# Bidirectional gated DeltaNet scan on one core: the second direction's operands moved to the other half of the partitions, its products queued in turn with the first's, and the state scaling on GpSimd

## The chip, the cores and the metric

The kernel runs on one core of one Trainium2 chip. The metric is device time in microseconds of one launch; the time before the change is the median of three runs.

## The reference

One layer of a hybrid model: 512 latent tokens and 256 context tokens of width 1024 go through a modulated RMS norm and one wide input projection, then through two mixers side by side (windowed attention, and a bidirectional gated delta rule), a gated merge, an output projection and a squared-ReLU MLP. All is fp32. The change is in the delta rule, cut to what matters:

```python
def gated_delta_chunked(q, k, v, g_log, beta, s0):
    # chunks of 64 tokens, 8 heads of 64; per chunk: G = cumsum(g), T = I + b * decay * k k^T
    ...
    def step(S, xs):
        w_c, uv_c, qd_c, intra_c, kt_c, gl_c = xs
        u = uv_c - jnp.einsum('bhck,bhkv->bhcv', w_c, S)
        o = jnp.einsum('bhck,bhkv->bhcv', qd_c, S) + jnp.einsum('bhij,bhjv->bhiv', intra_c, u)
        S = jnp.exp(gl_c)[..., None, None] * S + jnp.einsum('bhck,bhcv->bhkv', kt_c, u)
        return S, o
```

It runs forward and, on flipped inputs, backward; first over the 4 context chunks from a zero state, then over the 8 latent chunks from the states reached. The outputs of the two directions are added. So there are 12 steps, each of them one after the other, with two directions that do not depend on each other.

## The kernel before

Weights come from memory in 512 KB tiles, are split into a high and a low part (line 259 on ScalarE, line 266 on VectorE), and each large product is done as three matmuls. Between these large products the kernel runs the smaller ones of attention and of the delta rule.

A latent tile of state, values or products holds 128 partitions by 256 columns: the 8 heads are four columns of blocks (q = 0 to 3) by two halves of the partitions (64 each). A small product takes its two operands from one half of the partitions and writes to one half of a PSUM bank.

`chain_step(d, step)` is one step of one direction d, a generator with three phases:

- phase 0: the state products z = k S and, in latent steps, q S (line 1152), then R = z * eG - v / 2 on VectorE (lines 1156, 1157);
- phase 1: u = (inverse) R (line 1164), then uk = u * tb on VectorE (line 1170) and, in latent steps, a copy `us` (line 1174) and the scaled readout `zq` of q S (line 1176, one per head column) on ScalarE;
- phase 2: the new state's products (line 1185) and the inner outputs (line 1189), the old state scaled by its decay on ScalarE (line 1199, one per head column), the new state on VectorE (line 1201), and the output sums (lines 1208 to 1215).

`steps` runs the two directions phase by phase: all of direction 0's phase, then all of direction 1's. Between phases the caller puts other matmuls, the fill: `filler()` makes the attention branch's products (line 1073) and 14 gate tiles of 24 matmuls (line 1028), 432 matmuls in all. In the context scan, `weave` mixes the steps with the inverse of the latent chunks' matrices (`invert`, lines 856 and 857 on VectorE), 144 fill matmuls, and `rest` (normalising the queries, turning values and keys token-major). Then four transposes (`back`, line 867) and two `combine`s (lines 877 and 887, results copied at 896 to 899, zeros by GpSimd at 900 and 901) finish the latent inverses XA, and the query products (line 777) with VectorE, ScalarE and GpSimd (lines 1278 to 1289) make the masks IA; 144 fill matmuls stand between. The latent scan follows with `FILL[3]` = 8, 7 and 3 fill matmuls after the phases 0, 1 and 2.

`late_mod` makes 32 rows of the second modulation (line 1094, one VectorE product over a 512 KB tile each); `run_late` calls it in many places, in the latent scan once per step. `tok_major` (line 915) writes the token-major values VTM and keys KTM.

The order on each engine is fixed when the program is built: by program order, except that an instruction whose inputs are not ready by the builder's own estimate of the times is passed by later ones that are. Every engine then runs its queue in order. `add_manual_dep` adds an order to that without a wait.

## Time and profile before

| | us |
|---|---|
| median of 3 runs (911.4 to 913.39) | 912.83 |
| profiled execution | 911.22 |
| its span | 909.5 |
| TensorE matmul busy | 879.4 (97%) |
| VectorE busy | 585.4 (64%) |
| ScalarE busy | 454.9 (50%) |
| GpSimd busy | 25.2 (3%) |

The two scans, with what lies between them, take the stretch from 294 to 467 us of the span. In rows of the profile, "L1164" is line 1164 of the kernel, `x32` is a count of instructions, the first number of a row in order of time is its start in the span, the second its length, and `[0.74 <-DVE m L1157]` says that the engine stood idle for 0.74 us until that instruction released it. Each small fp32 product of 64x64x64 leaves two matmul records, so the 16 products of line 1164 in one step (8 per direction) are 32 records, and the 32 of line 1152 in a latent step are 64. In a table of stretches each row gives start:end, length, and the busy time of each engine with the number of instructions.

### The profile page before, as it was taken

Reading aid. Unit: us, or ns where it says so; the run is one execution under the profiler, and the core shown is the slowest. Engines: PE = TensorE matmul, PEld = TensorE weight load, DVE = VectorE, ACT = ScalarE, POOL = GpSimd, SP = SyncE. Lnnn points to the kernel's source line nnn. Section 1 sums busy time; section 2 is a strip of 40 time slices with the busy share of each in tenths; the row PEclk is TensorE's granted clock in tenths of the full one; section 3 lists DMA queues with packets and bytes.
Section 4 is the critical chain, followed back from the end, with each engine's and each line's share of the span. In section 5 each row is a group of like instructions: output and inputs, shape, how many; then the busy total and the mean of one; then the engine's idle time right before and its main releaser. Section 6 shows DMA issues by size and latency. Waiting matters only on the chain.

```text
span 909.5 us, 16844 instructions
## 1 busy us (share of the span) xinstructions
PE 879.4 (97%) x7082; PEld 704.7 (77%) x7082; DVE 585.4 (64%) x999; ACT 454.9 (50%) x819; POOL 25.2 (3%) x40
## 2 busy tenths in 40 slices
PE   8999999999899999999999999999999999999998
PEld 5668777867677787777678789888888888888886
DVE  3578799887778997677867988941654335324511
ACT  6588755476568786465663445630452134113400
POOL 0010001010000002010000000000000000000000
PEclk9999999999999999999999999999999999999999
DMA  8671455533001133633316773640553224322111
GB/s 355 262 230 21 92 117 120 112 71 58 13 13 35 56 110 94 207 98 95 117 37 219 245 245 135 227 144 1 188 157 95 70 73 150 103 69 79 38 47 46
DMA packets 30460, 105.59 MB, mean 116 GB/s; under 512 B 3760, under 2 KB 4400, under 8 KB 29360
## 3 DMA queue, kind: packets, MB, share of 16 engines
q1 hardware_dynamic: 28368, 97.18, 33.1%
q0 software_dynamic: 2016, 7.34, 5.0%
q8 instruction: 55, 0.90, 0.4%
q14 instruction: 21, 0.17, 0.1%
HBM read 102.41 MB, written 2.10 MB: 115 GB/s over the span
## 4 chain that ended last, share of the span: by engine, by line
PE 80%; DVE 10%; ACT 5%; issue 2%; DMA 1%; SPq 0%; DVEq 0%; ACTq 0%
PE banks L319 16%; PE banks L317 16%; PE banks L318 16%; PE banks L1028 9%; PE banks L424 5%; PE banks L1073 2%; PE banks L429 2%; PE banks L586 2%; PE banks L596 1%; PE banks L1164 1%; ACT m L148 1%; PE banks L662 1%; PE banks L1185 1%; PE banks L1152 1%; PE banks L210 1%
## 5 line engine op out<-in xcount | busy, mean ns | idle before, releaser
L317 PE MATMUL banks<-m,m 128*128 128x512 f32 (+1 forms) x600 | 223.6, 377 | 2.6 <-DVE m L643 1.6
L318 PE MATMUL banks<-m,m 128*128 128x512 f32 (+1 forms) x600 | 224.5, 376 | 0.1
L319 PE MATMUL banks<-m,m 128*128 128x512 f32 (+1 forms) x600 | 224.2, 376 | 0.0
L259 ACT ACTIVATE m<-wr 128x1024 fp32r<-128x1024 f32 x68 | 71.8, 1059 | 155.1 <-PE banks L318 74.0
L317 PEld LDWEIGHTS banks<-m,m 128*128 128x128 f32 x600 | 111.8, 188 | 26.0 <-ACT m L323 2.8
L318 PEld LDWEIGHTS banks<-m,m 128*128 128x128 f32 x600 | 112.5, 188 | 21.9 <-DVE m L324 1.5
L319 PEld LDWEIGHTS banks<-m,m 128*128 128x128 f32 x600 | 112.4, 188 | 21.3 <-issue 1.2
L266 DVE TENSOR_TENSOR m<-wr,m 128x1024 fp32r<-128x1024 f32 x68 | 82.8, 1224 | 62.8 <-ACT m L259 31.2
L1028 PE MATMUL banks<-m,wh 128*128 128x512 f32 x320 | 104.5, 405 | 1.5 <-issue 0.8
L1471 DVE SCALAR_TENSOR_TENSOR m<-banks,modT,m 128x512 f32<-128x512 f32 x32 | 24.0, 750 | 105.3 <-PE banks L319 105.3
L259 ACT ACTIVATE wh<-wr 128x1024 fp32r<-128x1024 f32 (+1 forms) x58 | 54.6, 941 | 50.6 <-issue 11.4
L424 PE MATMUL banks<-m,wh 128*128 128x512 f32 (+1 forms) x320 | 75.9, 374 | 1.2 <-DVE m L823 1.2
L1028 PEld LDWEIGHTS banks<-m,wh 128*128 128x128 f32 x320 | 58.0, 188 | 14.2 <-issue 1.0
L1028 PE MATMUL banks<-m,wl 128*128 128x512 f32 x160 | 64.7, 405 | 0.0
L424 PEld LDWEIGHTS banks<-m,wh 128*128 128x128 f32 x320 | 53.0, 189 | 11.5 <-issue 1.9
L266 DVE TENSOR_TENSOR wl<-wr,wh 128x1024 fp32r<-128x1024 f32 (+1 forms) x44 | 45.2, 1028 | 16.6 <-ACT wh L259 16.5
L184 ACT ACTIVATE m<-m 128x512 fp32r<-128x512 f32 (+1 forms) x56 | 34.8, 629 | 38.1 <-DVE m L1454 21.5
L185 DVE TENSOR_TENSOR m<-m,m 128x512 fp32r<-128x512 f32 (+1 forms) x56 | 38.3, 689 | 21.6 <-ACT m L184 21.3
L1094 DVE SCALAR_TENSOR_TENSOR m<-wa,m 128x1024 f32<-128x1024 f32 x32 | 39.0, 1223 | 12.6 <-DMA wa<-in_wada 7.4
L317 PE MATMUL banks<-m,wh 128*128 128x512 f32 (+1 forms) x120 | 42.0, 352 | 0.0
L319 PE MATMUL banks<-m,wl 128*128 128x512 f32 (+1 forms) x120 | 42.0, 351 | 0.0
L318 PE MATMUL banks<-m,wh 128*128 128x512 f32 (+1 forms) x120 | 41.8, 349 | 0.0
(241 smaller groups left out, 1371.8 us busy)
## 6 DMA issues: line engine op xcount, KB each, us to landing
wr<-in_wm SPq DMA_DIRECT2D x64, 512.0 KB, 3.7
wr<-in_win SPq DMA_DIRECT2D x38, 512.0 KB, 3.7
wa<-in_wada SPq DMA_DIRECT2D x32, 512.0 KB, 4.1
m<-in_wada SPq DMA_DIRECT2D x8, 1024.0 KB, 12.3
wl<-in_win POOLq DMA_DIRECT2D x14, 512.0 KB, 5.7
m<-in_xT SPq DMA_DIRECT2D x8, 512.0 KB, 5.6
wr<-in_wbr SPq DMA_DIRECT2D x16, 256.0 KB, 2.6
wr<-in_wout SPq DMA_DIRECT2D x8, 512.0 KB, 4.6
```

The costliest lines, as they stand in the source:

```text
L184: A.activation(r32(hi), src, AF.Copy)
L185: (eng or V).tensor_tensor(r32(lo), src, hi, op=ALU.subtract)
L259: h = A.activation(r32(hi), raw, AF.Copy)
L266: V.tensor_tensor(r32(lo), raw, hi, op=ALU.subtract)
L317: PE.matmul(acc, w[0][:, k, :], xhi, start=(start and i == 0), stop=False)
L318: PE.matmul(acc, w[0][:, k, :], xlo, start=False, stop=False)
L319: PE.matmul(acc, w[1][:, k, :], xhi, start=False, stop=(stop and i == n - 1))
L424: PE.matmul(a, w[0][:, k, :], x, start=(k == 0 and x is xs[k][0]), stop=False)
L429: PE.matmul(a, w[1][:, k, :], xs[k][0], start=False, stop=(k == KT - 1))
L1028: PE.matmul(acc.ap, w[x][:, k, :], hx[k][y], start=(k == p == 0), stop=(k == KT - 1 and p == 2))
L1094: V.scalar_tensor_tensor(t.ap, wa, 0.5, scr.ap, op0=ALU.mult, op1=ALU.mult, accum_out=modT[:, grp, j:j + 1])
L1471: V.scalar_tensor_tensor(xn_[ct], acc.ap, modT[:, 3, ct:ct + 1], xn_[ct], op0=ALU.mult, op1=ALU.add)
```

## The change

- Direction 1's inverses (`XAb` in `combine`) are written to the other half of the partitions; its values come from a copy `VTS` of the values with the halves exchanged (`swapped`, two DMAs on GpSimd's queue for each group of four chunks); z of k S and R lie in the other half too (`r2[i ^ x ^ d]`, `eGs` for direction 1). u, uk, the state and the outputs stay where they were.
- The products of line 1164, and in context steps those of line 1152, are yielded one head column at a time, so direction 0's and direction 1's stand in turn in the queue. In latent steps the state products stay together per direction.
- Since direction 1's q S now lies in the half where it does not belong, its readout is eight ScalarE operations of 64 partitions instead of four of 128.
- The scaling of the old state is one GpSimd product of 128x256, issued right after R, instead of four ScalarE operations in phase 2.
- In the second half of the latent steps the sum of the two directions' outputs, its squares and their sum are done after phase 1 of the next step (`add_up`). These sums and the rows of `late_mod` are ordered behind the last chain operation on VectorE (`behind`, `mark`). `late_mod` writes in place.
- `FILL[3]` becomes 7, 6, 5; the first latent phase 0 goes before the second group of query products; the latent scan makes four late rows instead of eight, two come after the gate tiles and six instead of four in the branch products; `rest` turns the values before it normalises the queries; the context scan is preceded by the exchanged copy and 12 fill matmuls. In `combine` direction 1's own columns are always copied.

```diff
-FILL = 144, 36, 36, (8, 7, 3)
+FILL = 144, 36, 36, (7, 6, 5)
...
         for a in range(2):
             lo, hi = quad(a, 0), quad(a, 1)
+            blo, bhi = quad(1 - a, 0), quad(1 - a, 1)
             A.activation(XAf[hi, :, HC:], XTf[hi], AF.Copy)
-            A.activation(XAb[hi, :, HC:], XTb[hi], AF.Copy)
+            A.activation(XAb[blo, :, :HC], XTb[lo], AF.Copy)
+            A.activation(XAb[bhi, :, HC:], XTb[hi], AF.Copy)
             A.activation(XAf[lo, :, HC:], xo[lo], AF.Copy)
-            A.activation(XAb[hi, :, :HC], xo[hi], AF.Copy)
+            A.activation(XAb[bhi, :, :HC], xo[hi], AF.Copy)
...
+    def swapped(g):
+        VTS[g] = alloc(1024, True)
+        for a in range(2):
+            G.dma_start(out=VTS[g][64 * a:64 * a + 64], in_=VTM[g][64 * (1 - a):64 * (1 - a) + 64])
...
-            t = alloc(1024)
-            V.scalar_tensor_tensor(t.ap, wa, 0.5, scr.ap, op0=ALU.mult, op1=ALU.mult, accum_out=modT[:, grp, j:j + 1])
-            t.free()
+            op = V.scalar_tensor_tensor(wa, wa, 0.5, scr.ap, op0=ALU.mult, op1=ALU.mult, accum_out=modT[:, grp, j:j + 1])
+            behind(op)
...
-        vt = VTM[c // 4][:, c % 4 * 256:(c % 4 + 1) * 256]
-        if S is not None:
-            for q in range(4):
+        vt = (VTS if d else VTM)[c // 4][:, c % 4 * 256:(c % 4 + 1) * 256]
+        for q in range(4):
+            if S is not None:
                 for x, src in enumerate((kT, qT) if lat else (kT,)):
                     for i, r in enumerate(r2):
-                        PE.matmul(z[r2[i ^ x], x * 512 + q * HD:x * 512 + (q + 1) * HD], src[q][r, col(c):col(c) + CH],
+                        PE.matmul(z[r2[i ^ x ^ d], x * 512 + q * HD:x * 512 + (q + 1) * HD], src[q][r, col(c):col(c) + CH],
                                   S[r, q * HD:(q + 1) * HD], start=True, stop=True)
+            if not lat:
+                yield
...
-            V.tensor_tensor(hv(R), hv(z[:, 0:256]), bc(eG[:, d, m4], HD), op=ALU.mult)
-            V.scalar_tensor_tensor(R, vt, -0.5, R, op0=ALU.mult, op1=ALU.add)
+            V.tensor_tensor(hv(R), hv(z[:, 0:256]), bc((eGs if d else eG)[:, d, m4], HD), op=ALU.mult)
+            mark[0] = V.scalar_tensor_tensor(R, vt, -0.5, R, op0=ALU.mult, op1=ALU.add)
+            if not last:
+                se = alloc(256)
+                G.tensor_tensor(hv(se.ap), hv(S.ap), bc(egl[:, d, m4], HD), op=ALU.mult)
...
-            for r in r2:
-                PE.matmul(u[r, q * HD:(q + 1) * HD], XA[lat][d][r, (cl * 4 + q) * CH:(cl * 4 + q + 1) * CH],
-                          R[r, q * HD:(q + 1) * HD], start=True, stop=True)
+            for i, r in enumerate(r2):
+                rr = r2[i ^ d]
+                PE.matmul(u[r, q * HD:(q + 1) * HD], XA[lat][d][rr, (cl * 4 + q) * CH:(cl * 4 + q + 1) * CH],
+                          R[rr, q * HD:(q + 1) * HD], start=True, stop=True)
+            yield
...
-                A.activation(zq[:, q * HD:(q + 1) * HD], z[:, 512 + q * HD:512 + (q + 1) * HD], AF.Copy,
-                             scale=eGs[:, d, c * 4 + q:c * 4 + q + 1])
+                for o, r in ((r2[1], r2[0]), (r2[0], r2[1])) if d else ((slice(0, P),) * 2,):
+                    A.activation(zq[o, q * HD:(q + 1) * HD], z[r, 512 + q * HD:512 + (q + 1) * HD], AF.Copy,
+                                 scale=(eG if d else eGs)[r, d, c * 4 + q:c * 4 + q + 1])
...
-                se = alloc(256)
-                for q in range(4):
-                    A.activation(se[:, q * HD:(q + 1) * HD], S[:, q * HD:(q + 1) * HD], AF.Copy,
-                                 scale=egl[:, d, c * 4 + q:c * 4 + q + 1])
...
+    def behind(op):
+        if mark[0]:
+            tc.add_manual_dep(op.ins, mark[0].ins.name, nosync, reason="behind the chain")
+
+    def add_up():
+
+        while after:
+            dst, b, cl = after.pop(0)
+            behind(V.tensor_tensor(dst, dst, b.ap, op=ALU.add))
+            A.activation(b.ap, dst, AF.Square)
+            V.tensor_reduce(oss[:, cl], hv(b.ap), axis=AX.X, op=ALU.add)
+            b.free()
...
-            for _ in range(3):
-                for g in both:
-                    next(g, None)
+            for n, parts in enumerate((1 if step >= NCC else 5, 5, 1)):
+                for _ in range(parts):
+                    for g in both:
+                        next(g, None)
+                if n == 1:
+                    add_up()
                 yield
...
+    swapped(0)
     to_tokens(KTM, kT, 0)
+    run_fill(12)
...
+        if g:
+            run_both(FPAUSE)
+            next(scan)
+        run_both(FILL[2] - (1 + g) * FPAUSE)
...
-    for n, _ in enumerate(steps(range(NCC, NC_))):
+    for n, _ in enumerate(scan, 1):
         run_fill(FILL[3][n % 3])
-        if n % 3 == 2:
+        if n % 3 == 1 and n < 3 * NCL // 2:
             run_late(1)
...
+    run_late(2)
     H.free()
...
-        run_late(ct % 2)
+        run_late(ct < 6)
```

More of the change, by code (lines that the diff above doesn't have):

```diff
@@ L917, in tok_major @@
             pt.free()
-    KTM, VTM = [None] * 3, [None] * 3
+    KTM, VTM, VTS = [None] * 3, [None] * 3, [None] * 3
     qT = []
@@ L1220, in steps @@
             both = [chain_step(d, step) for d in range(2)]
-            for _ in range(3):
-                for g in both:
-                    next(g, None)
+            for n, parts in enumerate((1 if step >= NCC else 5, 5, 1)):
[4 more added lines that the diff above has]
+                    add_up()
                 yield
+        add_up()
     def rest():
-        for q in range(4):
-            l2n(qT[q].ap, HD ** -0.5, ((0, SEQ),), epsc4)
-            yield
         for g in (1, 2):
@@ L1234, in rest @@
             t.free()
+        for q in range(4):
+            l2n(qT[q].ap, HD ** -0.5, ((0, SEQ),), epsc4)
+            yield
         for g in (1, 2):
@@ L1243, in tile_layer @@
         pass
-    for b in KTM[:1] + VTM[:1] + XA[0]:
+    for b in KTM[:1] + VTM[:1] + VTS[:1] + XA[0]:
         b.free()
@@ L1253, in tile_layer @@
         xr.append(alloc(1024))
-        back(xa[d][:, :, :HC], 1 + d, d == 1)
-        back(v3(xr[d].ap), 1 + d, d == 0)
+    xr.append(alloc(1024))
+    xr3 = [v3(b.ap) for b in xr]
+    back(xa[0][:, :, :HC], 1, False)
+    back(xr3[0], 1, True)
+    back(xr3[2], 2, True)
+    back(xr3[1], 2, False)
     X[1][0].free()
-    xr3 = [v3(b.ap) for b in xr]
     for g in range(2):
@@ L1265, in tile_layer @@
         b.free()
+    swapped(1)
+    swapped(2)
     IA = [alloc(2048, True), alloc(2048, True)]
+    scan = steps(range(NCC, NC_))
     ia = [v64(b.ap) for b in IA]
@@ L1302, in tile_layer @@
         pass
-    for b in kT + qT + KTM[1:] + VTM[1:] + XA[1] + IA + zb + Sb[0] + Sb[1]:
+    for b in kT + qT + KTM[1:] + VTM[1:] + VTS[1:] + XA[1] + IA + zb + Sb[0] + Sb[1]:
         b.free()
```

18 lines of the change are left out of this document (8 added, 10 removed).

## The prediction

> **What bounds the kernel now.** I read the page first, then the table of the stages around the two scans, then the chain of work that ended last and the order of time inside single steps. The page says who carries the span.
>
> ```profile
> span 909.5 us, 16844 instructions
> PE 879.4 (97%) x7082; PEld 704.7 (77%) x7082; DVE 585.4 (64%) x999; ACT 454.9 (50%) x819; POOL 25.2 (3%) x40
> PE 80%; DVE 10%; ACT 5%; issue 2%; DMA 1%; SPq 0%; DVEq 0%; ACTq 0%
> ...
> wl<-in_win POOLq DMA_DIRECT2D x14, 512.0 KB, 5.7
> ```
>
> TensorE carries it, so only two things count: less TensorE work, or fewer holes between its instructions. The scans lie in these stretches: context scan, combines and query products, latent scan, and what follows.
>
> ```profile
> 294.00:354.30 60.30, 59.88 (x556) 46.04 (x556) 56.53 (x106) 48.85 (x110) 2.24 (x5) 1.00 0.28 84
> 354.30:394.30 40.00, 39.33 (x893) 31.22 (x892) 22.54 (x33) 19.92 (x35) 5.49 (x10) 1.00 0.53 164
> 394.30:467.00 72.70, 67.15 (x1402) 51.78 (x1393) 53.86 (x123) 44.13 (x150) 1.48 (x2) 1.00 0.31 95
> ```
>
> Columns after the length: busy time of PE, PEld, DVE, ACT, POOL, then the granted clock (1.00 throughout). The context scan has TensorE and VectorE full at once (59.88 and 56.53 of 60.30); the latent scan has TensorE with 5.5 us of open holes, and VectorE at 74%. The chain prices the products:
>
> ```profile
> 308.91 1.08 PE banks L1152 x32
> ...
> 346.80 7.63 PE banks L1028 x32
> ...
> 360.79 4.85 PE banks L1028 x20
> ...
> 408.07 1.08 PE banks L1164 x32
> ...
> 413.41 1.09 PE banks L1152 x64
> ...
> 424.06 2.07 PE banks L1028 x8
> 426.13 1.08 PE banks L1164 x32
> 427.21 1.82 PE banks L1028 x7
> ...
> 453.21 1.08 PE banks L1164 x32
> ...
> 474.71 11.38 PE banks L1028 x49
> ```
>
> The reader should see that 64 records and 32 records cost the same. The 64 (state products of a latent step, L1152) use all four pairings of input half and output half; the 32 (L1164, and L1152 in the context steps) use only two, each half onto itself. So a pairing is a lane, and two lanes stand empty in L1164. A latent step without holes is 1.09 + 2.07 + 1.08 + 1.82 + 1.09 (new state and outputs, also 64 records) + three fill matmuls (0.78 at the rate of the seven) = 7.9 us. Measured from the L1164 at 408.07 to the one at 453.21, five steps take 45.14, or 9.03 each: 1.1 us of holes per step, some 9 us in eight steps.
>
> **The change part by part.**
>
> *Lanes, latent scan.* The second direction's inverses, values and R lie in the other half, and its L1164 products are queued one head after another with the first's: all four pairings in one stretch. 64 records' worth of lanes for 32 + 32: each step's L1164 goes from 1.08 to 1.09 / 2 = 0.54. Eight steps: **-4.3 us**. Nothing hides this; it is TensorE's own time. Bounds 0 (no overlap at all) and -4.3. I take the full value, because L1152 already shows the four-lane rate with the same sizes.
>
> *Lanes, context scan.* Four L1164 and three L1152 groups, 7 x 0.54 = 3.8 us of TensorE. But VectorE sets the end there: the inverse's two-input products (L856, L857) and four transposes lead into the first combine.
>
> ```profile
> L857 DVE TENSOR_TENSOR m<-m,m x60: 191/398/656, 138.1 to 341.4; 128x168 f32<-128x168 f32 x4, 128x30 f32<-128x30 f32 x2, 128x58 f32<-128x58 f32 x2, 128x84 f32<-128x84 f32 x2
> 351.89 2.12 DVE L867 STREAM_TRANSPOSE m<-m 128x1024 f32<-128x1024 f32 x1
> ```
>
> The last transpose ends at 354.0; the 32 fill matmuls from 346.80 end at 354.43, just when the combine's products can start. A TensorE that arrives 3.8 us earlier waits for VectorE, unless later fill is pulled ahead (it was in the latent scan: the code asks for 8, 7, 3 and single steps ran 8, 8, 2). VectorE has 3.8 us idle in this stretch (60.30 - 56.53). I take **-1.0**, nearer to the VectorE row; bounds -3.8 and, if GpSimd gets in its way (rival below), +4.2.
>
> *Holes by late modulation rows.* L1094 takes 1.22 us of VectorE in the middle of the chain:
>
> ```profile
> 441.64 1.22 DVE L1094 SCALAR_TENSOR_TENSOR m<-wa,m 128x1024 f32<-128x1024 f32 x1
> 443.12 0.74 DVE L1156 TENSOR_TENSOR m<-banks,eg 128x256 f32<-128x256 f32 x2
> 444.25 1.15 PE L1164 MATMUL banks<-m,m 64*64 64x64 f32 x32 [0.74 <-DVE m L1157]
> ...
> 461.23 1.22 DVE L1094 SCALAR_TENSOR_TENSOR m<-wa,m 128x1024 f32<-128x1024 f32 x1
> 462.37 0.42 DVE L1157 SCALAR_TENSOR_TENSOR m<-m,m 128x256 f32<-128x256 f32 x1
> 462.85 0.68 PE L1164 MATMUL banks<-m,m 64*64 64x64 f32 x16 [0.35 <-DVE m L1157]
> ```
>
> At 441.64 it stands ahead of R and TensorE sits 0.74; at 461.23 it splits R of the second direction and costs 1.22 less the 0.68 of the first direction's products. After the change four instead of eight are in the scan, each ordered behind the last chain operation, as are the output sums, which move one phase on. Behind uk they have the run of six fill matmuls plus the first half of the 64 records, some 2.2 us, before VectorE is wanted. Bounds 0 and -3.0 (four hits of about 0.75); I take **-2.0**. The four moved rows (and four more 512 KB loads later) lie beside the gate tiles' 49 matmuls and the branch products, TensorE unbroken for 11.38 us; without that cover they cost 4 x 1.22 = 4.9. The in-place product frees arena space and costs the same 1.22.
>
> *State scaling to GpSimd, output scaling doubled for one direction.*
>
> ```profile
> 412.69 2.02 ACT L1199 ACTIVATE m<-m,egl 128x64 f32<-128x64 f32 x8 [0.82 <-DVE m L1201]
> 414.62 1.71 ACT L1176 ACTIVATE m<-banks,eGs 128x64 f32<-128x64 f32 x8
> 418.65 0.79 ACT L1174 ACTIVATE m<-banks 128x256 f32<-128x256 f32 x2 [2.32 <-DVE m L1170]
> 379.47 0.73 PE L1028 MATMUL banks<-m,wh 128*128 128x512 f32 x2 [0.67 <-ACT m L148]
> 388.79 1.06 ACT L259 ACTIVATE wh<-wr 128x1024 fp32r<-128x1024 f32 x1
> 397.86 0.74 POOL L1288 MEMSET m<- 32x512 f32 x1 [10.00 <-DVE m L1285]
> ```
>
> ScalarE loses eight L1199 (2.02 us per step) and gains four L1176 (half of 1.71, 0.86). The loss frees the hole of 0.67 at 379.47, where eight L1199 from 375.8 held up the weight split and the tanh behind it: **-0.7**, bounds 0 and -2.0. The gain lies where it is wanted: twelve L1176 (2.57) and two L1174 (0.79) must end before the new state's products, 1.82 + 0.54 + 1.6 = 4.0 us after the state products. That leaves 0.6 us; a weight split (1.06) that falls in there, with its tanh (0.6), overruns by 1.0. Six tiles, some of them twice unlucky: **+2.0**, bounds 0 and 8 x 0.86 = +6.9.
>
> The GpSimd product (128x256, two inputs) has no row here. Nearest rows: 0.74 for its memset of 512 elements, 0.42 for VectorE's 128x256 product. I take 0.7. It starts when the state is there and is wanted a whole step later (7 us, two products 1.4): **0** in the latent scan as long as one product stays under 3 us; above that each microsecond costs two per step.
>
> *Ahead of the scans.* The swapped values come by DMA on POOL's queue behind sixteen evictions.
>
> ```profile
> 293.57 6.31 ACT L915 ACTIVATE m<-banks 64x256 f32<-64x256 f32 x16
> 294.10 1.04 PE L1164 MATMUL banks<-m,m 64*64 64x64 f32 x16 [0.89 <-ACT m L915]
> ...
> 299.47 0.68 PE L1164 MATMUL banks<-m,m 64*64 64x64 f32 x16
> ```
>
> The eight of the values end near 296.7; with the queue's 5.7 us (bound from above, those are 512 KB from memory; here 256 KB in two) the first L1164 starts at 301 to 303 instead of 294.1 and 299.5. Twelve more fill matmuls (2.8 us) and eight transposes of the reordered rest stand before it; behind it on POOL waits only the first state product, wanted at 318. **+0.5**, bounds 0 and +3. The four later DMAs have 30 us to land. Five more copies in the combines (0.6 each) lie under 20 fill matmuls, 4.85 us; without that cover 3.0.
>
> *Start of the latent scan.* Its first state products now go before the second half of the query products, so R no longer waits for the masks' building, but uk does.
>
> ```profile
> 395.48 1.28 DVE L1278 TENSOR_TENSOR m<-m,banks 128x512 f32<-128x512 f32 x2
> 397.39 1.83 DVE L1285 COPY m<-m 32x512 f32<-32x512 f32 x4
> 400.48 1.15 PE L1164 MATMUL banks<-m,m 64*64 64x64 f32 x32 [1.74 <-DVE m L1157]
> ```
>
> VectorE needs 1.28 + 0.68 + 1.83 = 3.8 us there; TensorE has 0.54 + 1.6 us before it wants uk, where before it had 13 fills and lost 1.74. **+0.5**, bounds -1.7 and +2.3.
>
> The sum: -4.3 - 1.0 - 2.0 - 0.7 + 2.0 + 0.5 + 0.5 = **-5.0 us**. The profiled execution took 911.22 (span 909.5), 1.6 under the median 912.83; from 911.22 the sum gives 906.2, and the same difference on the median **907.8**. About 1.8 us (0.2%) is what the runs can tell from no change.
>
> **The rivals.**
>
> *All of it stays.* The lanes give 4.3 + 3.8, pulled-ahead fill covers VectorE in the context scan, and 6 of the 9 us of holes go: -14, **899**. For it: every hole named has VectorE or ScalarE work in front of it that is moved. Against it: the filled VectorE of the first stretch, and L266, which is not ordered behind the chain and at 434.26 split R just as L1094 did.
>
> *GpSimd gets in VectorE's way (slower).* Place: the state product beside VectorE operations with two inputs from SBUF: L856/L857 in the context scan, R's second operation and L266 in the latent one. Price: if each holds VectorE for its own 0.7 us, 6 x 0.7 = 4.2 on the full VectorE ahead of the combine and 14 x 0.7 = 9.8 in the chain; with the first whole and a third of the second on the path, +7.5: **915**; all of it, 922. It decides from 0.25 us per product (5.0 / 20) on. For it: VectorE has no slack in the first stretch, and the order on TensorE is fixed ahead of time. Against it: POOL ran only memsets and DMA issues there, so the trace has no overlap to show; and in the latent scan the product would run beside the state products, when VectorE idles. The Trainium skill has the rule behind this rival: SBUF — State Buffer, "Who interferes with whom", says that a VectorE instruction with two SBUF inputs contends with a GpSimd instruction that reads SBUF and that the loser blocks for the whole instruction. No run so far shows it. The skill's GPSIMD Engine Reference, "Elementwise — side-by-side cycle accounting", gives about 2.6 cycles per element for two inputs, which is an estimate of 0.55 us plus dispatch for 256 elements; by it the full price would be 11 us, not 14.
>
> *The lanes are given back.* With the directions in turn, the first direction's uk waits for the second direction's R, so L1170 no longer overlaps the products; a step would lose on VectorE (0.42 + 0.42 after the products) what TensorE saved, and ScalarE's twelve readouts take the rest: -4.3 falls away, **912**. For it: R of both takes 1.5 us (four operations, 0.74 a pair) against 1.82 of cover, so any insertion breaks it. Against it: six fills (1.6) stand behind L1164, and uk for both (0.74, as two L1156 of that size), the second copy (half of 0.79) and some 0.3 of latency are 1.45.
>
> **How the numbers follow.** The forecast (903 to 911.0) 0.57; all of it 0.15; GpSimd 0.15; given back 0.13. Faster by over 0.2% (under 911.0): 0.57 + 0.15 = 0.72; within 0.2%: 0.13; slower: 0.15. The range 898.5 to 915.5 reaches the first rival's time and the smaller price of the second; outside lie about half of the GpSimd case and a few hundredths below. The forecast's own range is 903 to 911.
>
> **What would show it.** L1164's stretch at 0.54 us for 32 records, and L1152 likewise in the context steps (right); 1.08 in both (given back at the root). The five-step pace at about 8.3 to 8.5 us, where 7.5 would be all of it and 9 none. No L1094 between L1201 and L1157. In the first stretch, TensorE idle ahead of L877 with L867 as the releaser, 2 to 3 us. The POOL products at 0.5 to 0.9 us each; VectorE's L856/L857 grown in mean above 0.39 and 0.40 us would be contention. I am wrong if the latent scan's TensorE holes grow (waits of L1185 on ScalarE L1176 or L1174 over 3 us in sum), or if the new state waits for GpSimd.

## The result

The changed kernel is slower: 920.28 us (median of 6 runs, 919.46 to 925.19) against 912.60 us of the kernel before, timed beside it (910.39 to 914.42); ratio 1.0089 (95% interval 1.0072 to 1.0106). The forecast was 907.8, with 898.5 to 915.5 as its range. The profiled execution took 919.46 us.

The page after, with the rows that answer to those of before:

```profile
span 917.7 us, 16870 instructions
...
PE 880.7 (96%) x7082; PEld 702.6 (77%) x7082; DVE 587.3 (64%) x999; ACT 452.7 (49%) x776; POOL 42.4 (5%) x66
...
PE 74%; DVE 13%; ACT 7%; issue 3%; DMA 3%; SPq 0%; DVEq 0%; ACTq 0%
```

TensorE's busy time is 1.3 us up although its small products use two lanes more; that is the clock (below), since an execution of nearly the same kernel at full clock (e6) has 876.8. In the chain ScalarE and the DMA have each gained 2 points.

The next fence is the table of stretches after: context scan (from its first product to the first combine), combines and query products (to the last query product), latent scan (to the last inner outputs); then from the last fill matmul to the first matmul of the second norm, and from there to the last of it. Line 1157 after is line 1152 before, 1164 and 1165 are 1156 and 1157, 1176 is 1164, 1183 is 1170, 1187 is 1174, 1190 is 1176, 1199 is 1185, 1203 is 1189, 1099 is 1094, 1034 is 1028; 1168 is the new product on GpSimd.

```profile
296.49:360.98 64.49, 61.15 (x568) 45.63 (x568) 60.95 (x110) 44.55 (x88) 10.38 (x15) 1.00 0.34 99
360.98:406.00 45.02, 42.26 (x956) 32.99 (x956) 22.06 (x35) 23.80 (x43) 7.20 (x13) 0.96 0.51 160
406.00:469.70 63.70, 60.79 (x1332) 45.83 (x1320) 48.10 (x111) 42.51 (x121) 8.82 (x14) 1.00 0.25 77
488.96:558.62 69.66, 66.82 (x344) 55.78 (x343) 58.37 (x92) 27.68 (x39) 0.00 (x0) 1.00 0.81 262
558.62:569.04 10.42, 9.83 (x74) 9.34 (x75) 10.15 (x23) 5.58 (x12) 0.00 (x0) 1.00 0.26 72
```

And the same stretches of the kernel before, cut at the same events:

```profile
294.10:354.37 60.27, 59.95 (x557) 46.01 (x557) 56.50 (x106) 48.82 (x110) 2.31 (x5) 1.00 0.28 84
354.37:394.21 39.84, 39.17 (x893) 31.17 (x892) 22.47 (x33) 19.76 (x34) 5.42 (x10) 1.00 0.53 164
394.21:466.22 72.01, 66.46 (x1405) 51.21 (x1393) 53.12 (x121) 44.22 (x150) 1.48 (x2) 1.00 0.32 96
485.70:552.10 66.40, 66.38 (x347) 56.04 (x346) 55.92 (x87) 27.04 (x38) 0.00 (x0) 1.00 0.76 247
552.10:561.39 9.29, 8.95 (x69) 8.45 (x68) 9.17 (x22) 5.75 (x13) 0.00 (x0) 1.00 0.20 56
```

The latent scan is 8.3 us shorter and the two stretches ahead of it are 4.2 and 5.2 longer: 12 fill matmuls (2.8 us) and a group of state products (1.2 us) were moved into them, and the granted clock of the second is 0.96. The three together are 1.1 us longer. What is lost beyond doubt stands further down: behind the scans, where the change touches only the late rows and the placing of buffers, 66.40 us have become 69.66 and 9.29 have become 10.42. A further 2.4 us are lost ahead of the scans (first product of line 1176 at 296.49 instead of 294.10); e6 below, whose only further edit lies behind the scans, does not lose them.

One latent step after, and the start of the same product five steps later:

```profile
420.77 0.61 POOL L1168 TENSOR_TENSOR m<-m,egl 128x256 f32<-128x256 f32 x1
...
422.98 2.56 ACT L1190 ACTIVATE m<-banks,eg 64x64 f32<-64x64 f32 x8
...
424.15 0.69 PE L1176 MATMUL banks<-m,m 64*64 64x64 f32 x32
424.78 0.73 PE L1034 MATMUL banks<-m,wh 128*128 128x512 f32 x2
...
426.18 1.06 ACT L259 ACTIVATE wh<-wr 128x1024 fp32r<-128x1024 f32 x1
...
427.36 0.33 PE L1199 MATMUL banks<-m,m 64*64 64x64 f32 x4 [0.92 <-ACT wh L259]
...
466.18 0.69 PE L1176 MATMUL banks<-m,m 64*64 64x64 f32 x32
```

The 32 records of line 1176 now leave TensorE after 0.63 us (424.15 to 424.78) instead of 1.08, and five steps take 42.03 us, 8.41 each instead of 9.03. They do so in six of the eight latent steps. In the other two the products of the two directions stand apart or mostly behind one another, and take 1.22 us (two times 0.61) and 1.24:

```profile
415.79 0.68 PE L1176 MATMUL banks<-m,m 64*64 64x64 f32 x16
...
448.86 1.31 PE L1176 MATMUL banks<-m,m 64*64 64x64 f32 x32
```

So the pace forecast for the latent scan (8.3 to 8.5 us) came true, and the named sign of being wrong, growing holes there, did not appear: TensorE's open time in the latent scan fell from 5.55 us (72.01 less 66.46) to 2.91. The rest of this document is about where those microseconds went.

### The profile page after: what moved, and what is told of

The parts are those of the page before. It is cut to its first block, busy times and chain, and to the rows that moved or that the text cites. A ratio compares the mean times of both kernels' runs of the same rounds, so it can differ in the third digit from the quotient of the medians.

```text
span 917.7 us, 16870 instructions
## 1 busy us (share of the span) xinstructions
PE 880.7 (96%) x7082; PEld 702.6 (77%) x7082; DVE 587.3 (64%) x999; ACT 452.7 (49%) x776; POOL 42.4 (5%) x66
## 4 chain that ended last, share of the span: by engine, by line
PE 74%; DVE 13%; ACT 7%; issue 3%; DMA 3%; SPq 0%; DVEq 0%; ACTq 0%
PE banks L317 15%; PE banks L319 15%; PE banks L318 15%; PE banks L1034 9%; PE banks L424 5%; PE banks L429 2%; PE banks L586 2%; PE banks L596 1%; DVE wl L266 1%; ACT m L1190 1%; DMA wr<-in_wm 1%; DVE m L867 1%; DVE m L857 1%; ACT m L916 1%; PE banks L1199 1%
## 5 line engine op out<-in xcount | busy, mean ns | idle before, releaser
L266 DVE TENSOR_TENSOR m<-wr,m 128x1024 fp32r<-128x1024 f32 x68 | 83.2, 1224 | 79.6 <-PE banks L318 44.4
L1099 DVE SCALAR_TENSOR_TENSOR wa<-wa,m 128x1024 f32<-128x1024 f32 x32 | 38.8, 1220 | 15.8 <-DMA wa<-in_wada 15.8
```

Source lines behind the costliest of these rows:

```text
L266: V.tensor_tensor(r32(lo), raw, hi, op=ALU.subtract)
L1099: op = V.scalar_tensor_tensor(wa, wa, 0.5, scr.ap, op0=ALU.mult, op1=ALU.mult, accum_out=modT[:, grp, j:j + 1])
```

## The experiments

All ratios are to the kernel before, timed beside each kernel. "Clean" below means a profiled execution in which the granted clock was not lowered ahead of its last two microseconds (before, e3, e6, e8, e16 and e17). Lengths "to the last fill matmul" start at the first product of u (line 1176 after, 1164 before), those "to the end" stop at the end of the span.

### What is lost behind the scans

**e1_late_rows**: the late rows are called where they were.

```diff
-        if n % 3 == 1 and n < 3 * NCL // 2:
+        if n % 3 == 1:
             run_late(1)
...
-    run_late(2)
     H.free()
...
-        run_late(ct < 6)
+        run_late(ct % 2)
```

> The changed kernel with the late modulation rows where they were: one in each of the eight latent steps (still ordered behind the chain), none after the gate tiles, four in the branch products. Theory P (the loss is a sum of parts, and the largest lies behind the scans, where two more 512 KB rows in the branch products and two after the gate tiles take slots and turns from the weight loads): the shift of the products from the scan's end to the second norm falls from about 5 us to about 1, four more rows of 1.22 us in the scan cost at most 1, so 916 to 917 on the before median of 912.6. Rival G (GpSimd's product holds VectorE and all else follows): the late rows don't matter, 920.

918.82 us, 1.0075 (1.0055 to 1.0095): less than expected, and not told apart from the changed kernel. ScalarE no longer waits for the branch weights (4.5 us in the changed kernel, next experiment), and yet it takes 69.15 us from the last fill matmul to the first norm instead of 69.66.

**e6_x_elsewhere**: in the changed kernel the buffer of the residual's x lies inside the 32 arena units of the modulated input, since the arena's free units have shifted; here it lies in units that the output norms release.

```diff
-    X1 = alloc(8 * SEQ, True)
+    mem.used[62:78] = [True] * 16
+    X1 = Buf(mem, 62, 16, mem.at(62 * mem.unit, 8 * SEQ))
```

> The changed kernel with one buffer placed elsewhere: the residual's x (16 units of the arena) lies in units 62 to 77, which the output norms release, and no longer inside the 32 units of the modulated input, which the last gate matmul releases. Nothing else is changed. Theory M (the change moved this buffer into the input's region, so its four loads wait for the gate matmuls and then stand between the branch weights' loads): the loads are issued at about 482 instead of 489 to 499, ScalarE no longer waits for the branch weights (4.5 us before the norm), and the stretch from the last fill matmul to the first norm falls from 69.7 to about 67: 917 us. Rival N (the loads' order doesn't matter, the branch stretch is longer because of the two more late rows and their loads): the stretch stays at 69 to 70 and the time at 920.

919.29 us, 1.0065 (1.0041 to 1.0089). The loads moved to 482 to 492 us as expected, but ScalarE waits for the branch weights as in the changed kernel. First the changed kernel's row, then the stretches of this one (context scan, between the scans, latent scan, and the two behind the fill) and its row:

```profile
ACT wh L259 <- DMA wr<-in_wbr: 4.5, 2, 2.3
```

```profile
294.24:358.72 64.48, 61.14 (x569) 45.65 (x569) 60.94 (x110) 44.54 (x88) 10.37 (x15) 1.00 0.34 99
358.72:402.71 43.99, 40.67 (x956) 32.09 (x956) 22.13 (x35) 23.80 (x42) 7.21 (x13) 1.00 0.55 161
402.71:466.42 63.71, 60.81 (x1331) 45.87 (x1321) 48.08 (x111) 42.52 (x121) 8.82 (x14) 1.00 0.26 78
485.70:554.69 68.99, 66.64 (x345) 55.64 (x343) 58.25 (x92) 27.76 (x39) 0.00 (x0) 1.00 0.78 254
554.69:565.12 10.43, 9.84 (x75) 9.35 (x76) 10.16 (x23) 5.59 (x12) 0.00 (x0) 1.00 0.30 89
```

```profile
ACT wh L259 <- DMA wr<-in_wbr: 4.4, 2, 2.5
```

So x's place is not what ScalarE waits for; the late rows' loads are (e1). This execution (915.58 us, granted clock 0.999) is a clean look at the change: its last fill matmul starts at 485.70, where it stands in the kernel before. All that the change gained and lost up to the end of the scans cancels there; the 4.4 us by which this execution is longer than 911.22 lie behind.

**e12_late_and_x**: both edits at once.

> The changed kernel with two things as before at once: x lies outside the input's region, and the late rows are called where they were (one per latent step, four in the branch products). Theory L (the four late rows moved behind the scan bring four more 512 KB loads into the stretch after it, where the weights' loads already set the pace; either cause alone was enough to delay them): from the last fill matmul to the first norm 66.4 to 67 us again instead of 69, ScalarE waits for the branch weights under 1 us, and the time falls to 914.5 to 916. Rival N (that stretch is longer for another reason): 69 us and 918 to 919.

917.19 us, 1.0052 (1.0032 to 1.0073), and 68.05 us in that stretch: between the two theories. Late rows and x together are worth 0.0037 of 912.7, 3.4 us, with intervals that just touch. In the two profiled executions the way from the last fill matmul to the end is 1.5 us shorter (428.74 to 427.28), while the rows, back in the scans, take 0.7 us there (192.47 to 193.19 to the last fill matmul). Nearly 5 us are still missing, part of them around the norm, where the profile shows late rows (line 1099) on VectorE between the residual's operations. That led to the in-place write: without a buffer to wait for, a late row is ready earlier by the builder's estimate, and it is put ahead.

**e16_readout_on_vector** (e12 with another readout, below) and **e17_rows_not_in_place** (the same, with the late rows behind the scans written to an arena buffer again):

```diff
+            t = alloc(1024) if behind_scan else None
-            op = V.scalar_tensor_tensor(wa, wa, 0.5, scr.ap, ...)
-            behind(op)
+            op = V.scalar_tensor_tensor(t.ap if t else wa, wa, 0.5, scr.ap, ...)
+            if t:
+                t.free()
+            else:
+                behind(op)
```

> As e16_readout_on_vector, and behind the scans the late rows are written to a buffer of the arena again, as before the change, not in place. Theory I (in place a late row waits for no arena buffer, so the builder puts it ahead of the residual's operations and the norm's on VectorE, and TensorE stands still around the norm): from the last fill matmul to the first norm 66.5 to 67.2 us instead of 68.8, from the first to the last norm 9.3 to 9.8 instead of 11.4, and the time 911.5 to 913: no slower than the kernel before, perhaps a little faster. Rival D (the loads' pace sets this stretch): no change, 915 to 916.5.

912.94 us, 0.9995 (0.9984 to 1.0006), against 1.0039 for e16: the in-place write cost 4 us (the edit also leaves out the order behind the chain's last operation, which is long done there). From the last fill matmul to the end the two clean executions take 429.00 us (e16) and 424.33 (e17). VectorE around the norm, and the two stretches, in e16:

```profile
548.94 1.23 DVE L1099 SCALAR_TENSOR_TENSOR wa<-wa,m 128x1024 f32<-128x1024 f32 x1 [0.93 <-DMA wa<-in_wada]
...
553.92 1.23 DVE L1099 SCALAR_TENSOR_TENSOR wa<-wa,m 128x1024 f32<-128x1024 f32 x1 [1.29 <-DMA wa<-in_wada]
...
555.41 1.67 DVE L322 SCALAR_TENSOR_TENSOR m<-m,mA,m 128x256 f32<-128x256 f32 x4
```

```profile
483.90:552.69 68.79, 67.37 (x347) 55.75 (x345) 56.98 (x89) 28.03 (x39) 0.00 (x0) 1.00 0.76 249
552.69:564.13 11.44, 9.82 (x74) 9.34 (x75) 10.21 (x23) 5.70 (x12) 0.00 (x0) 1.00 0.28 78
```

and in e17:

```profile
551.61 1.22 DVE L1101 SCALAR_TENSOR_TENSOR m<-wa,m 128x1024 f32<-128x1024 f32 x1
...
554.23 1.27 DVE L322 SCALAR_TENSOR_TENSOR m<-m,mA,m 128x256 f32<-128x256 f32 x3
```

```profile
485.27:551.76 66.49, 66.47 (x347) 56.02 (x346) 55.87 (x88) 27.08 (x39) 0.00 (x0) 1.00 0.76 248
551.76:561.82 10.06, 8.87 (x69) 8.48 (x68) 10.06 (x23) 6.57 (x14) 0.00 (x0) 1.00 0.33 106
```

In e16 two rows whose loads have not landed stand ahead of the norm's first operation (line 322) and VectorE waits for the DMA in front of it; in e17 the row ahead of it doesn't wait for its load, and the stretch from the fill to the first norm is 66.49 us, that of before, the next 1.4 us shorter.

### What the exchange costs and brings

**e13_four_readouts**: e6 with four readouts instead of eight for direction 1. This leaves out the exchange of the halves in the readout, so direction 1's outputs are added to the wrong half; every other instruction stays.

```diff
-                for o, r in ((r2[1], r2[0]), (r2[0], r2[1])) if d else ((slice(0, P),) * 2,):
+                for o, r in ((slice(0, P),) * 2,):
```

> The changed kernel with x elsewhere (e6_x_elsewhere) and the second direction's readout done as four operations of 128 partitions, which leaves out its exchange of the halves (the outputs of that direction are then added to the wrong half); every other instruction stays. Theory R (the doubled readouts eat what the lanes gave: twelve operations on ScalarE hold up the copy, the weight split and its tanh): the holes ahead of L1199, 3.05 us in e6_x_elsewhere, fall under 1 us, the stretch from the first to the last inner outputs gets 2 to 3.5 us shorter and so does the end of the fill: 916 to 917. Rival V (the latent scan is paced by VectorE's chain, and ScalarE's work lies beside it): no change, 918.5 to 919.5.

914.44 us, 1.0022 (1.0011 to 1.0033), against 1.0065 for e6: by the ratios the doubled readouts cost 3.9 us. Some of that is the clock: its mean over the runs is 0.9962 in e6 and 0.9982 here, and in the profiled executions, from the first product of u to the end, where neither clock is lowered, the two are 1.9 us apart (619.56 and 617.67). The gain is not at the place expected: the holes ahead of line 1199 fell only from 3.05 to 2.29 us (1.66 of that is in the context scan), but the one at the start of the latent scan fell from 2.25 to 0.42. In the changed kernel it reads:

```profile
395.37 0.93 ACT L1190 ACTIVATE m<-banks,eGs 128x64 f32<-128x64 f32 x4
...
396.31 2.56 ACT L1190 ACTIVATE m<-banks,eg 64x64 f32<-64x64 f32 x8
...
398.89 1.06 ACT L259 ACTIVATE wh<-wr 128x1024 fp32r<-128x1024 f32 x1
...
399.97 0.60 ACT L148 ACTIVATE m<-banks 128x512 f32<-128x512 f32 x1
...
400.62 0.73 PE L1034 MATMUL banks<-m,wh 128*128 128x512 f32 x2 [2.25 <-ACT m L148]
```

```profile
402.00:405.00 3.00, 3.00 (x12) 1.87 (x12) 0.00 (x0) 0.00 (x0) 0.00 (x0) 0.50 0.60 214
```

Twelve readouts of 3.49 us hold up the split and the tanh behind them, TensorE waits 2.25 us for a free bank, and then, the last row says, TensorE has a granted clock of 0.50 for 3 us. With four readouts there is no such stretch; nor is there one in e6's profile, which has the same hole (2.25 us at 398.85).

**e16_readout_on_vector**: e12, and direction 1's readout as two VectorE products of 64x256.

```diff
+            if d:
+                for o, r in ((r2[1], r2[0]), (r2[0], r2[1])):
+                    V.tensor_tensor(hv(zq[o]), hv(z[r, 512:768]), bc(eG[r, d, m4], HD), op=ALU.mult)
```

> As e12_late_and_x, and the second direction's readout is done by two VectorE products of 64 partitions by 256 columns, after uk, instead of eight ScalarE operations of 64 by 64. Theory R: the holes ahead of L1199 go as in the four-readout kernel, and as VectorE is busy for three quarters of the latent scan the two products (about 0.4 us each) lie beside the fill: 2 us under e12_late_and_x, 912.5 to 914. Rival V (VectorE sets the pace there, and two more products per step put 6 us on it): slower than e12_late_and_x by 2 to 6.

915.73 us, 1.0039 (1.0025 to 1.0054), 1.2 us less than e12 by the ratios, whose intervals overlap. The fill ends 1.8 us earlier than in the kernel before; the rest was the norm (above).

**e7_queries_first**: the first latent state products behind the query products, as before the change.

> The changed kernel with the first latent state products behind the query products again, as before the change; all else stays. Theory H (at the start of the latent scan twelve readouts on ScalarE stand ahead of a weight split and its tanh, so TensorE stands still for 2.25 us, and the granted clock drops to half right behind that hole): the hole at 400.6 us and the drop go, and the stretch from the end of the second combine to the first inner outputs, 30.4 us in the changed kernel less the moved products, gets 2 to 3.5 shorter: 917 to 918. Rival W (R then waits for the mask building as before, 1.74 us, and the readouts meet the split all the same): no gain, 919.5 to 921.

922.08 us, 1.0101 (1.0082 to 1.0120): a miss. The twelve readouts then stand ahead of the copy of u (line 1187) and the split, and TensorE waits 1.24 us for R and 1.15 us for that copy.

**e3_own_halves**: no exchange (`d` replaced by 0 in every choice of a half, no `VTS`); the rest of the change stays. **e8_own_halves_x** adds x elsewhere, **e9_own_halves_x_ctx_scalar** adds to that the scaling on ScalarE in the context steps.

> The changed kernel with the second direction's values, inverses and R left in their own half (no exchanged copy, no extra copies in the combines, four readouts per direction instead of eight), the products still queued in turn. Theory P: the latent scan loses the 4.3 us of the lanes (a group of 32 records takes 1.08 instead of 0.62), and gets back 1.8 us in the first combine, 1.5 at the scan's start and 0.5 in the context scan: 920 to 922. Rival S (the exchange and its copies and readouts are the loss): 912 to 914 in spite of the lanes.

> The kernel with both directions in their own halves (no exchange; still queued in turn, scaling on GpSimd) and with the residual's x placed in units 58 to 73, released by the output norms. Theory M: the 3.5 us that the own-halves kernel loses behind the scans go, 912.5 to 913.5, no different from the kernel before. Rival N: 916.

> As the own-halves kernel with x elsewhere, and the state is scaled on ScalarE in the context steps, on GpSimd in the latent steps alone. Theory G (in the context scan the GpSimd products slow VectorE's two-input products, which set its end; in the latent scan they help): 1.2 us less than the kernel beside it, 911 to 912.3, and L856 and L857 sum to about 28.2 us again instead of 29.4. Rival F (the context scan's 37.9 us are set elsewhere): the same as the kernel beside it, within 0.5.

916.13 (1.0038, 1.0025 to 1.0052), 916.59 (1.0043, 1.0026 to 1.0059) and 917.19 us (1.0046, 1.0030 to 1.0062). The first lies between its two theories. By the ratios the exchange as built is a loss of 4.7 us (1.0089 less 1.0038), though it makes TensorE's products shorter. Little of that is in the order of the work: the clean executions of e3 and e6, which has the exchange, have spans of 913.2 and 913.8 us. About 2 us go with the clock (means 0.9978 and 0.9953, see below). Neither addition did anything: x's place is worth nothing here, against what theory M said, and neither is GpSimd's absence from the context scan, although it does slow VectorE. In the changed kernel the longest of line 857's products is 1049 ns instead of 656, beside GpSimd's own products (line 1168):

```profile
L857 DVE TENSOR_TENSOR m<-m,m x60: 191/400/1049, 139.2 to 345.4; 128x168 f32<-128x168 f32 x4, 128x30 f32<-128x30 f32 x2, 128x58 f32<-128x58 f32 x2, 128x84 f32<-128x84 f32 x2
...
L1168 POOL TENSOR_TENSOR m<-m,egl x20: 604/612/1528, 311.8 to 454.1; 128x256 f32<-128x256 f32 x20
```

**e4_latent_only**: the exchange in the latent scan alone.

> The changed kernel with the other half used in the latent scan alone: the context steps and the first combine as before the change, no exchanged copy of the context values. Theory P: VectorE sets the end of the context scan, so the lanes there bought nothing, and the first combine's 1.8 us and 1 to 2 us at the context scan's start come back: 916.5 to 918. Rival L (the context scan's lanes are worth their 3.8 us and only late rows and GpSimd lose): 922 to 924.

924.78 us, 1.0136 (1.0115 to 1.0158), near the time of the second theory, but not for its reason: without the lanes the context scan has the same length (64.64 us against 64.49), so in this kernel they are worth nothing there. The hole behind the twelve readouts is there too (2.26 us at 401.8), and 9.29 us between the norm's first and last matmul became 13.7. TensorE waits 2.06 us for ScalarE in that stretch (at 564.3), and the granted clock drops behind it; why ScalarE is late there was not settled.

**e18_own_halves_mended**: e8 with the late rows called and written as before behind the scans.

> Both directions in their own halves, with x elsewhere, the late rows called where they were and not in place behind the scans; left of the change are the turn in the queue, the scaling on GpSimd, the later output sums, the fill's 7, 6, 5 and the order ahead of the scans. Theory I: what the own-halves kernels lost behind the scans goes, 911 to 913; the pair with e17 then gives the worth of the exchange with its readout on VectorE, 0 to 2 us in favour of the exchange. Rival D: 915 to 917.

913.62 us, 1.0016 (1.0003 to 1.0029): 2.5 us less than e8, so the late rows cost time without the exchange too; and 1.9 us (by the ratios) more than e17, which has it, as the first theory said. From the first product of u to the end, where neither clock is lowered, the profiled executions are 1.2 us apart (616.30 and 615.12).

**e19_no_fill_ahead** (e17 without the 12 fill matmuls ahead of the scans), **e20_mended** (the same with x in units that are released early in that kernel) and **e21_mended_own_halves** (e20 without the exchange):

> As e17_rows_not_in_place, without the 12 fill matmuls ahead of the context scan (they are used later). Theory C (they only move TensorE work: VectorE sets the end of the context scan, and the fill that they take is missing later): the same as e17 within 0.8. Rival K (they cover the DMA of the exchanged values: without them the first product of the second direction waits and the whole scan starts 1 to 2 us later): slower by 1 to 2.

> As e19_no_fill_ahead, with x in units 78 to 93, which the output norms release in that kernel. Theory C (without the 12 matmuls ahead the fill ends 2.4 us earlier than in the kernel before, and the loss behind it was the x loads' place alone): from the last fill matmul to the first norm 66.4 to 67 us instead of 71.2, and the time 910 to 911.5: 2 us faster than the kernel before. Rival B (the stretch behind is set by the weights' loads, which don't come earlier): 912.5 to 914.

> As e20_mended with both directions in their own halves, their readouts on ScalarE and x in units 91 to 106, which the output norms release here. Lane theory (the exchange saves 2 to 4 us of TensorE in the latent scan, of which part comes back as waits): 1 to 2 us slower than e20_mended. Rival Z (the exchange is worth nothing once TensorE waits for VectorE's chain): the same as e20_mended within 0.6.

e19: 913.50 us, 1.0011 (0.9996 to 1.0026), near e17 but not for the reason given: its last fill matmul starts 2.35 us before that of the kernel before, and the loss came behind it, where the four loads of x were issued at 506 us, ahead of the output weights' (its 62 to 77 are released late in this kernel). e20: 910.65 us, 0.9983 (0.9972 to 0.9994). e21: 909.89 us, 0.9982 (0.9971 to 0.9993). Both beat the kernel before by 1.6 us, and the runs do not tell them apart (in the pair e17 and e18 the exchange was worth 1.9 us). Their latent scans, their stretches behind the fill, and the matmul behind the second norm's first wait read (e20, then e21):

```profile
397.92:461.38 63.46, 61.13 (x1331) 46.41 (x1320) 58.37 (x132) 24.80 (x66) 8.82 (x14) 1.00 0.35 116
482.93:549.41 66.48, 66.46 (x347) 55.99 (x346) 55.89 (x87) 27.04 (x38) 0.00 (x0) 1.00 0.70 231
...
552.98 0.63 PE L317 MATMUL banks<-m,m 128*128 128x256 f32 x3 [1.08 <-ACT m L323]
```

```profile
398.88:463.20 64.32, 63.08 (x1331) 48.72 (x1320) 52.58 (x119) 30.51 (x94) 8.80 (x14) 1.00 0.37 117
484.70:551.88 67.18, 66.76 (x347) 56.19 (x346) 55.73 (x87) 26.68 (x38) 0.00 (x0) 1.00 0.72 233
...
554.71 0.62 PE L317 MATMUL banks<-m,m 128*128 128x256 f32 x3 [0.37 <-ACT m L323]
```

With the exchange TensorE is busy for 2.0 us less and the scan is 0.9 us shorter; VectorE works 5.8 us more. In these executions e20 comes to the second norm 2.5 us before e21 (549.41 and 551.88) and loses most of it there: its stretch from the norm's first to its last matmul takes 11.31 us instead of 9.31, and TensorE's first wait in it is 1.08 us instead of 0.37. From the first product of u to the end 1.0 us is left (612.85 and 613.80). So the exchange, with its readout on VectorE, gains about 1 us in both pairs of executions, which is too little for the runs to tell from nothing.

### The scaling of the state

**e2_scale_on_scalar**: the changed kernel with the state scaled on ScalarE again. **e15_gpsimd_latent_only**: the kernel before, with the GpSimd scaling in the latent steps alone.

> The changed kernel with the state scaled on ScalarE again, four operations per direction in the last phase, all else as changed. Rival G: VectorE's two-input operations are no longer held, the inverse runs at its old pace, the time falls to 912 to 914. Theory P: the inverse's operations lose 1.2 us in the context scan to GpSimd, no more, and ScalarE gets 2 us per latent step back beside the twelve readouts: 918 to 922.

> The kernel before with one part of the change alone: in the latent steps the state is scaled by one GpSimd product issued after R, instead of four ScalarE operations; in the context steps it stays on ScalarE. Theory S (eight ScalarE operations fewer per step in the latent scan are worth 2 us by themselves, as e2_scale_on_scalar shows from the other side): 910.5 to 911.5. Rival T (before the change ScalarE had time for them, and they only count together with the twelve readouts): 912.5 to 913.5.

923.08 us (1.0110, 1.0086 to 1.0134; the rival's 912 to 914 is excluded) and 912.22 us (1.0002, 0.9989 to 1.0015; rival T). Taken back from the changed kernel it costs 1.9 us by the ratios, whose intervals overlap, and 2.4 in the executions to the last fill matmul (193.82 against 191.46 in e6, no lowered clock in either); put into the kernel before it gains nothing. So it seems only to make room on ScalarE for the doubled readouts. In e2 the context scan, from its first state product to the first combine, is 1.3 us shorter than in the changed kernel (44.4 against 45.65), the price of GpSimd beside the full VectorE; the latent scan is longer by more. In e9 the same removal shortened nothing, so what that price is worth depends on what else ends the context scan.

## Why the prediction was wrong

The terms of the sum, with what was measured (the first three from profiled executions, the changed kernel or e6 against before; the others from the ratios of pairs, times 912.7, where nothing else is said, so some of the clock is in them):

| step | forecast | measured |
|---|---|---|
| lanes, latent scan | -4.3 | -2.4 (six stretches of 0.62 to 0.68 us and two of 1.22 and 1.24, for eight of 1.08) |
| lanes, context scan | -1.0 | 0: TensorE's 2.3 us came back as holes of 2.8 |
| holes by late rows, in the scan | -2.0 | -2.7 (all holes of the scan, 5.55 to 2.90 us; ahead of the products of u 3.92 to 0.20) |
| state scaling off ScalarE | -0.7 | 0 by itself (e15) |
| doubled readouts, start of the latent scan | +2.5 | +3.9 (e13 against e6), 1.9 of it at full clock |
| ahead of the scans | +0.5 | +1.1 (e20 against e17, where x lies elsewhere too; the intervals overlap) |
| late rows moved, beside gate matmuls | 0 | +1.6 in the stretch behind the fill (69.66 to 68.05, e12) |
| late rows in place | 0 | +4.0 (e17 against e16) |
| clock | none | about +2 |

The rows overlap and come from two kinds of measurement, so they do not add up to the loss. The stretches of the clean execution e6, less those of the kernel before, do; the 2.8 us of fill and 1.2 of state products that moved are counted where they stood:

| stretch | forecast | measured |
|---|---|---|
| up to the end of the context scan | -0.5 | +1.6 |
| between the scans | -0.2 | +3.0 |
| latent scan | -4.3 | -4.3 |
| rest of the fill | 0 | -0.2 |
| behind the last fill matmul | 0 | +4.3 |
| sum | -5.0 | +4.3 |

(The forecast column is the prediction's terms by place: -1.0 + 0.5; -0.7 + 0.5; -4.3 - 2.0 + 2.0.) The other 3.8 of the 8.1 us (0.0089 of 912.7) are not in that execution. About 2 of them go with the clock and 0.7 with x's place (69.66 against 68.99); the rest stays unassigned.

**The steps that failed behind the scans are two priced at nothing.** "The four moved rows (and four more 512 KB loads later) lie beside the gate tiles' 49 matmuls": they do, as far as VectorE goes, but their loads run between those of the branch weights, for which ScalarE then waits 4.5 us, and TensorE behind it 0.78 and 0.49 us. With the rows called where they were, ScalarE's wait is gone (e1, e12). The other step is "The in-place product frees arena space and costs the same 1.22". Its duration is the same. Its place is not: the old write waited for an arena buffer, and that wait kept the late rows behind the residual's operations. The run shows the cost; that the buffer's wait is what kept the rows back is read from the two orders on VectorE, and is not shown by itself. Nothing in a profile of before shows this; the prediction took the duration for the cost.

**The readouts were mispriced and misplaced.** The prediction put the twelve at 2.57 us, the price of twelve operations of 128 partitions. In the rows above four of 128 partitions take 0.93 us, 0.23 each, and eight of 64 take 2.56, 0.32 each: 3.49 together, and the 0.6 us that the prediction had to spare is gone. The cost came at another place: not at the six tiles in the middle of the scan, but at its start, where all twelve stand ahead of one weight split. That the +2.0 taken lies near the 1.9 measured at full clock is luck; the clock comes on top.

**The lanes** behaved as the row of line 1152 said where the directions stand in turn, at 0.63 instead of 0.54 us, but in two of the eight latent steps they do not; why was not settled. So a little over half of the 4.3 us came. That the latent scan's sum is right all the same is partly luck. Its holes were misread, too: "some 9 us in eight steps" were 5.55 by the prediction's own table of stretches. And the context part of the forecast had the answer, "VectorE sets the end there", and still took a gain. In the changed kernel the transposes go ahead of uk, and TensorE, early now, waits:

```profile
347.92 4.04 DVE L867 STREAM_TRANSPOSE m<-m 128x1024 f32<-128x1024 f32 x2
351.83 0.71 DVE L1183 TENSOR_TENSOR m<-banks,eg 128x256 f32<-128x256 f32 x2
...
352.26 1.15 PE L1199 MATMUL banks<-m,m 64*64 64x64 f32 x32 [1.65 <-DVE m L1183]
```

Another 1.15 us of holes stand ahead of the token turning (line 911), behind ScalarE's evictions.

**The rivals.** "All of it stays" had no support. "GpSimd gets in VectorE's way" was the forecast's only road to a slower kernel and named a time near the one measured, but not the cause: e2, without any GpSimd product, is no faster, and e9, with none in the context steps, is no faster than e8. The contention itself is there, 656 to 1049 ns, as the rule of the Trainium skill says (SBUF — State Buffer, "Who interferes with whom"); it cost 1.3 us of the context scan by e2, and nothing by e9. The 0.7 us taken for the GpSimd product measured 0.61. "The lanes are given back" fits e20 and e21 in part: of the 2.0 us that TensorE saves in the latent scan 0.9 are left, and most of the lead up to the second norm is lost at it. The wait that it named was not shown to be the reason.

**The clock** was in no step. In the profiled execution after, it falls to 0.50 twice, right behind TensorE holes of 2.09 and 2.25 us. The first stands in the kernel before too, with the same length. From the matmul behind that hole to the first product of u it takes 51.42 us after instead of 50.40, so the drop is 1.0 of the 2.4 us lost ahead of the scans. The other 1.4 were lost before it (245.07 against 243.70, last section), and e6 comes to that product at 294.24. The second hole is that of the readouts. Over the runs the mean granted clock was 0.994 to 0.996 for the changed kernel and 0.995 to 1.000 for the kernel before, and a straight line through all runs, with a level of its own for each kernel, gives about 0.8 us for 0.001. Between the means, 0.9953 and 0.9978, that is 2 us of the 8. It is a correlation, and no run varied the holes alone, but the kernels bear it out: the seven with twelve readouts on ScalarE (the changed kernel, e1, e2, e4, e6, e7 and e12) have mean clocks of 0.994 to 0.996, the eleven others (e13 among them) of 0.997 to 0.999.

## What to carry to other kernels

A moved or rewritten instruction has a cost beyond its duration: its loads, the buffer that it used to wait for, and its place in queues far downstream. Check in the trace after, stage by stage up to the end, that the stages which the change does not mean to touch still have their length; here the gains stood in the scans and most of the loss behind them. When a gain on the busiest engine is forecast, read first which engine ends the wait in that stretch: shorter TensorE work ahead of a full VectorE is only an earlier wait.

## What the runs showed of the hardware

The granted clock can halve behind a hole well under 3 us, and need not. Before and after have the same hole of 2.09 us in the same place; of these two profiles only the changed kernel's has the clock fall behind it. All 19 profiles have that hole, of 2.08 to 2.11 us, and in 10 of them a stretch at 0.50 follows it; of the six with a hole of 2.25 to 2.28 us at the start of the latent scan, four have a stretch at 0.50 behind that one. Two further drops (e1 at 17 us, e19 at 520) have no hole of over 1.5 us in front of them. The hole and the next 3 us, kernel before:

```profile
243.70 0.96 PE L586 MATMUL banks<-m,m 128*128 128x512 f32 x3 [2.09 <-DVE m L185]
```

```profile
244.00:247.00 3.00, 3.00 (x22) 2.51 (x20) 1.63 (x4) 1.80 (x3) 0.00 (x0) 1.00 0.01 3
```

Changed kernel:

```profile
245.07 1.22 PE L586 MATMUL banks<-m,m 128*128 128x512 f32 x2 [2.09 <-DVE m L185]
```

```profile
245.00:248.00 3.00, 2.93 (x10) 2.57 (x11) 0.85 (x4) 0.96 (x3) 0.00 (x0) 0.50 0.01 3
```

Of the same sequence 22 matmul records lie in the one stretch and 10 in the other. The Trainium skill (TensorE: Matmul & The Clock Gate, Part 1) puts the return to half clock at an idle window of about 3.4 us; the trace differs: two stretches at 0.50 follow holes of 2.09 and 2.25 us.
